# Squares, low parts and picks reordered between the last attention projection and the first expert

## The chip, the cores and the metric

The program runs on one core of one Trainium2 chip. The metric is the device time of one execution in microseconds (us), lower is better. A timed run starts the program once; the number quoted is the median of the runs.

## What is computed

A two-layer decoder over 512 tokens of width 1024. Layer 0 is a gated short convolution with a dense SwiGLU, layer 1 is latent attention with a mixture of eight experts, two for each token. The change stands where layer 1's attention ends and its experts begin; cut to that:

```python
x = x + mla_mixer(...)                      # ends with  o @ w_o
h = rmsnorm(x, norm_ffn[1])                 # x * rsqrt(mean(x*x) + eps) * g
probs = softmax(h @ router)                 # 8 logits per token
vals, idx = top_k(probs, 2)
gates = vals / sum(vals), scattered to (token, expert)
out = 0
for e in range(8):
    out = out + gates[:, e:e+1] * ((silu(h @ w_gate[e]) * (h @ w_up[e])) @ w_down[e])
x = x + out
```

## The kernel before, in words

Everything from line 404 on runs under a manual schedule: the order in which the code is written is the order in each engine's queue, and every engine works off its queue strictly in that order.

**Weights as chunks.** A class `Stream` brings the weights in as chunks of 128x2048 fp32 (1 MB each, `w_raw`, loaded by SP's queue into a ring of buffers). ScalarE (ACT) copies a chunk to a high part, `w_hi` (`split_hi`, L88), and VectorE (DVE) subtracts it from the raw chunk to get a bf16 low part, `w_lo` (`split_lo`, L97). A raw buffer is free for the next load once its low part is made. The first expert chunk alone, chunk 0, is split in eight pieces of 256 columns by the generator `pieces` (`split`, L117 on ACT and L120 on DVE), one piece for each pass of the loop below.

**The last output projection** (loop over `fo`, L877 to L895). `xT` holds x transposed, eight blocks of 128 features by 512 tokens. In each pass TensorE makes six products into a PSUM tile (`out_mm`, L688 to L690) and, two passes behind, the router's logits from the high and low parts `xhr` and `xlr` of that block (`logits`, L872 and L873). DVE adds the product to `xT` (L882), ACT copies it to `xhr` (L885), DVE makes the previous block's `xlr` (L888), ACT squares the block into `sq` (L891), GpSimd (POOL) adds the square to `acc` (L893), and one piece of chunk 0 is split. The last square is added by DVE behind the loop (L933).

**The router and the rows.** TensorE transposes `xT` back to rows of tokens, eight groups `rows_mm(0)` to `rows_mm(7)` (L909), the last ones placed between the router's steps. Each group is copied as it is to SBUF and stored to `out` (`base`, L921 and L922) and, scaled by the norm `r3`, split in a high part on ACT and a low part on DVE (`rows_ev`, L914 and L915; the tiles are called xh and xl in the profile). The norm comes from `acc`: TensorE sums over features (`pss`, L942), DVE makes `m4` (L1137), POOL raises it to the power -1/2 (L248). The logits are copied by ACT (`lgt`, L932), transposed on TensorE (L938) and ranked on DVE (L1139 to L1149) to the mask `sel`; products of `sel` with a triangular matrix (L1151, L1153) give each token's place in its expert (`pos`, L1159), and DVE turns expert 0's places into a one-hot matrix `oh1` (L1168). `keep_warm(n)` (L946) issues n products of ones that nobody reads.

**Picks.** For the first expert the tokens are picked by products: `pick(f, part)` (L1185 to L1190) multiplies the rows' high part (part 0) or low part (part 1) of feature block f with `oh1`, four products each, into one PSUM tile for each f. ACT and DVE evict it to `xe` (L1200, L1201). The PSUM pool `ops` has six buffers, shared by the loop's tiles, the rows and the picks, so a pick may have to wait until an older tile is read out. The later experts fetch their rows from memory (`hrow`), which POOL's queue writes (L1181).

**The experts** (L1319 on). Each chunk k gives 16 products with `w_hi` and 16 with `w_lo` (L1033). In the pass of chunk k, DVE first adds the two halves of the result (L1041) and then makes the low part of chunk k+2, besides the small work of ranking the experts and finding their rows.

## Time and profile before

| what | value |
|---|---|
| median of 3 runs | 1410.83 us (1410.05 to 1412.65) |
| the profiled execution | 1413.99 us |
| its span, first to last instruction | 1412.2 us |
| TensorE busy | 1378.1 us, 98% of the span |
| DVE busy | 991.5 us, 70% |
| ACT busy | 814.8 us, 58% |
| POOL busy | 281.2 us, 20% |
| mean granted TensorE clock | 0.993 of 2.4 GHz |

The span is the profiled execution from its first instruction to its last; the run's time has 1.8 us more around it. Busy shares are averages over all stages, and TensorE counts as busy while products follow each other, whatever its clock. The stage of the change is some 40 us of the 1412: the loop from 751 to 771 us, the router and the picks from 771 to 787, and the first chunks of the first expert behind it.

### The profile page before, as it was taken

Reading aid. Unit: us, or ns where it says so; the run is one execution under the profiler, and the core shown is the slowest. Engines: PE = TensorE matmul, PEld = TensorE weight load, DVE = VectorE, ACT = ScalarE, POOL = GpSimd, SP = SyncE. Lnnn points to the kernel's source line nnn. Section 1 sums busy time; section 2 is a strip of 40 time slices with the busy share of each in tenths; the row PEclk is TensorE's granted clock in tenths of the full one; section 3 lists DMA queues with packets and bytes.
Section 4 is the critical chain, followed back from the end, with each engine's and each line's share of the span. In section 5 each row is a group of like instructions: output and inputs, shape, how many; then the busy total and the mean of one; then the engine's idle time right before and its main releaser. Section 6 shows DMA issues by size and latency. Waiting matters only on the chain. (4 is left out here: it accounts for less than half of the span.)

```text
span 1412.2 us, 23783 instructions
## 1 busy us (share of the span) xinstructions
PE 1378.1 (98%) x9541; PEld 1198.7 (85%) x9544; DVE 991.5 (70%) x1263; ACT 814.8 (58%) x1210; POOL 281.2 (20%) x206
## 2 busy tenths in 40 slices
PE   9999999999999999999998999999999999999995
PEld 6888888888888887878876899999999999979893
DVE  7745564443344444586778897897979899999995
ACT  6323332221222233576645787877878788888892
POOL 0000000000000000143202432342523343443221
PEclk9999999999999999999999999999999999999998
DMA  6322223222232222111204999988999899999992
GB/s 222 135 92 90 90 90 119 90 90 90 95 114 90 90 90 92 64 35 58 91 0 162 309 366 370 311 324 289 357 321 343 340 348 368 318 399 359 402 375 70
DMA packets 49390, 284.40 MB, mean 201 GB/s; under 512 B 9320, under 2 KB 11112, under 8 KB 17272
## 3 DMA queue, kind: packets, MB, share of 16 engines
q1 hardware_dynamic: 41688, 269.82, 52.5%
q0 software_dynamic: 7584, 12.98, 3.9%
q8 instruction: 77, 1.26, 0.4%
q14 instruction: 41, 0.34, 0.1%
HBM read 271.39 MB, written 11.37 MB: 200 GB/s over the span
## 5 line engine op out<-in xcount | busy, mean ns | idle before, releaser
L97 DVE TENSOR_TENSOR w_lo<-w_raw,w_hi 128x2048 bf16<-128x2048 f32 (+1 forms) x239 | 555.7, 2326 | 54.2 <-ACT w_hi L88 54.2
L88 ACT CAST w_hi<-w_raw 128x2048 fp32r<-128x2048 f32 x239 | 456.4, 1910 | 216.3 <-PE ps L256 153.8
L1033 PE MATMUL gu<-xe,w_hi 128*128 128x304 f32 (+6 forms) x2048 | 288.8, 293 | 0.0
L1033 PEld LDWEIGHTS gu<-xe,w_hi 128*128 128x128 f32 x2048 | 264.0, 189 | 0.4
L255 PE MATMUL ps<-xh,w_hi 128*128 128x512 f32 x592 | 231.7, 391 | 1.6 <-DVE xT L399 0.9
L256 PE MATMUL ps<-xl,w_hi 128*128 128x512 f32 x592 | 230.5, 389 | 0.3 <-DVE xl L291 0.3
L257 PE MATMUL ps<-xh,w_lo 128*128 128x512 f32 x592 | 230.4, 389 | 0.0
L1047 POOL TENSOR_TENSOR sg<-sg,p 128x304 f32<-128x304 f32 (+6 forms) x64 | 93.8, 1465 | 310.8 <-ACT sg L1046 310.5
L1033 PE MATMUL gu<-xb,w_lo 128*128 128x152 bf16 (+6 forms) x2048 | 143.4, 223 | 3.8 <-DVE w_lo L97 3.7
L255 PEld LDWEIGHTS ps<-xh,w_hi 128*128 128x128 f32 x592 | 111.2, 188 | 26.0 <-ACT xh L290 1.4
L256 PEld LDWEIGHTS ps<-xl,w_hi 128*128 128x128 f32 x592 | 111.1, 188 | 24.3 <-DVE xl L291 0.8
L1033 PEld LDWEIGHTS <-w_lo 128*128 128x128 bf16 x2048 | 120.6, 98 | 12.8 <-DVE w_lo L97 5.6
L257 PEld LDWEIGHTS ps<-xh,w_lo 128*128 128x128 f32 x592 | 111.1, 188 | 23.1
L248 POOL TENSOR_TENSOR rs<-m,mhalf 128x4 f32<-128x4 f32 x3 | 3.1, 1019 | 589.2 <-DVE m L505 554.3
L1077 PE MATMUL gu<-ae,w_hi 128*128 128x304 f32 (+3 forms) x640 | 97.4, 302 | 0.0
L257 PE MATMUL ps<-ah,w_lo 128*128 128x512 f32 x240 | 94.7, 394 | 0.0
L256 PE MATMUL ps<-al,w_hi 128*128 128x512 f32 x240 | 94.6, 394 | 0.0
L255 PE MATMUL ps<-ah,w_hi 128*128 128x512 f32 x240 | 94.6, 394 | 0.0
L1077 PEld LDWEIGHTS gu<-ae,w_hi 128*128 128x128 f32 x640 | 87.1, 189 | 0.0
L1040 ACT COPY p<-gu 128x304 f32<-128x304 f32 (+6 forms) x128 | 49.1, 384 | 41.9 <-PE gu L1033 41.0
L1041 DVE TENSOR_TENSOR p<-gu,p 128x304 f32<-128x304 f32 (+6 forms) x128 | 55.5, 434 | 24.9 <-ACT p L1040 22.8
L968 POOL TENSOR_SCALAR oh<-rest,posn 128x152 bf16<-128x152 f32 (+6 forms) x28 | 58.0, 2084 | 1.3 <-DVE posn L1258 1.3
(334 smaller groups left out, 1875.9 us busy)
## 6 DMA issues: line engine op xcount, KB each, us to landing
w_raw<-w_moe SPq DMA_DIRECT2D x192, 1024.0 KB, 8.3
w_raw<-w_a SPq DMA_DIRECT2D x50, 1024.0 KB, 4.9
w_raw<-w_hp SPq DMA_DIRECT2D x4, 1088.0 KB, 5.9
w_raw<-w_o SPq DMA_DIRECT2D x4, 1024.0 KB, 4.7
xT<-xT_in SPq DMA_DIRECT2D x8, 256.0 KB, 4.8
out<-hs SPq DMA_DIRECT2D x8, 256.0 KB, 3.6
hrow<-xh POOLq DMA_DIRECT2D x2, 1024.0 KB, 5.9
hrow<-xl POOLq DMA_DIRECT2D x2, 1024.0 KB, 23.3
```

Source lines behind the costliest of these rows:

```text
L88: self.nc.scalar.copy(hi[:, :w], self.raw[k][:, :w])
L97: self.nc.vector.tensor_tensor(lo[:, :w], self.raw.pop(k)[:, :w], self.hi[k][:, :w].bitcast(F32), ALU.subtract)
L248: nc.gpsimd.tensor_tensor(out_t, m, h, ALU.pow)
L255: mm(ps, wh, xh[:, kc, :], start=kc == 0, stop=False)
L256: mm(ps, wh, xl[:, kc, :], start=False, stop=False)
L257: mm(ps, wl, xh[:, kc, :], start=False, stop=kc == n - 1)
L968: nc.gpsimd.tensor_scalar(s.oh[:, tb, 0:s.cap], iota[:, 0:s.cap], p[:, tb], None, op0=ALU.is_equal)
L1033: mm(s.ps[:, i, 0:n], w[:, b:b + P], x[:, kc], start=w is hi and kc == 0, stop=w is lo and kc == NB - 1)
L1040: nc.scalar.copy(p2, s.ps[:, :, s.cap:2 * s.cap])
L1041: tt(p2, s.ps[:, :, 0:s.cap], p2, ALU.add)
L1047: nc.gpsimd.tensor_tensor(s.sg, s.sg, s.p2[:, :, 1], ALU.mult)
L1077: mm(s.dp[q // 2][:, q % 2, 0:n], w[:, b:b + P], x[:, 4 * kq + j], start=w is hi and kq + j == 0, stop=w is lo and kq + j == 6)
```

## The change

It rewrites the order of this stage, in these edits:

1. In the loop the squares are added to `acc` by DVE and no longer by POOL. The eight pieces of chunk 0 are split to their high part alone (`split_hi_parts`); its low part is made in one operation behind the picks, ahead of chunk 1's.
2. The norm's sums stand ahead of the transposes of the logits. The copies `base(2)` and `base(3)` go from DVE to ACT; `rows_mm(4)` and `rows_mm(5)` move later.
3. Of twelve idle products three are left; those behind the products of `sel` are gone.
4. The picks run two feature blocks ahead and no longer one; `rows_ev(0)` goes ahead of `pos`, rows 7 and the rest of the rows behind the first two picks. ACT's high part of chunk 1 and the copies `base(4)` to `base(7)` stand together behind the last `rows_ev`. POOL's selection for expert 0 moves behind the first two stores to `hrow`, and `find(0)` one chunk later.

```diff
-    def split(self, parts=None, lag=False):
+    def split_hi_parts(self, parts):
...
+        for n in parts:
+            self.nc.scalar.copy(hi[:, a:a + n], self.raw[k][:, a:a + n])
+            a += n
+            yield
...
-    pieces = ws.split([256] * 8, True)
+    pieces = ws.split_hi_parts([256] * 8)
...
         if 0 < fo < NB - 1:
-            nc.gpsimd.tensor_tensor(acc, acc, sq, ALU.add)
-        if fo < NB - 1:
-            next(pieces)
+            tt(acc, acc, sq, ALU.add)
+        next(pieces)
...
-    rows_mm(4)
+    tt(acc, acc, sq, ALU.add)
+    for tb in range(TB):
+        t_s = slice(tb * P, (tb + 1) * P)
+        mm(pss[:, tb:tb + 1], acc[:, t_s], ones[:, 0:1], start=tb == 0, stop=tb == TB - 1)
     for i in range(2):
         base(i, nc.scalar.copy)
     lgt = ot.tile([2 * NE, T], F32, name="lgt", bufs=1)
     nc.scalar.copy(lgt, plt[0:2 * NE, :])
-    tt(acc, acc, sq, ALU.add)
-    for i in range(2, 4):
-        base(i, nc.vector.tensor_copy)
-    list(pieces)
     for tb in range(TB):
         nc.tensor.transpose(misc[:, tb * 2 * NE:(tb + 1) * 2 * NE], lgt[:, tb * P:(tb + 1) * P],
...
-    rows_mm(5)
+    for i in range(2, 4):
+        base(i, nc.scalar.copy)
+    rows_mm(4)
...
-    keep_warm(6)
-    ws.split_hi()
-    for i in range(4, 6):
-        base(i, nc.scalar.copy)
+    keep_warm(3)
...
     ts(sel_b, rank, 2.0, None, op0=ALU.is_lt)
+    rows_ev(0)
...
-    keep_warm(6)
+    rows_mm(5)
     rows_mm(6, idle)
...
-    ex[0].select(pos[:, :, 0:1])
...
-    for i in range(8):
+    for i in range(1, 4):
         rows_ev(i)
-        if i == 0:
-            rows_mm(7)
-    for i in (6, 7):
-        base(i, nc.scalar.copy)
...
     pick(0, 0)
+    pick(1, 0)
+    rows_mm(7)
+    for i in range(4, 8):
+        rows_ev(i)
+    ws.split_hi()
+    for i in range(4, 8):
+        base(i, nc.scalar.copy)
...
+        if part == 0:
+            ex[0].select(pos[:, :, 0:1])
     for f in range(NB):
-        if f < NB - 1:
-            pick(f + 1, 0)
+        if f < NB - 2:
+            pick(f + 2, 0)
         pick(f, 1)
...
+    ws.split_lo()
     ws.split_lo()
     ws.split_hi()
...
+                if c == 2:
+                    x.find(0)
                 if c == 1:
-                    x.find(0)
```

Three places of the engines' queues, before and then after. The first is DVE at the end of the loop over `fo`, from the sixth pass to the norm's `m`. Before:

```order
L120 TENSOR_TENSOR w_lo<-w_raw,w_hi 128x256 [waits Activation_49]
L882 TENSOR_TENSOR xT<-ps,xT 128x512 [waits PE_49]
L888 TENSOR_TENSOR xlr<-xT,xhr 128x512 [waits Activation_49]
L896 TENSOR_TENSOR xlr<-xT,xhr 128x512 [waits Activation_49]
L933 TENSOR_TENSOR acc<-acc,sq 128x512 [waits Activation_49,Pool_49]
L921 COPY hs<-ps 128x512 [waits PE_49] x2
L120 TENSOR_TENSOR w_lo<-w_raw,w_hi 128x256
L120 TENSOR_TENSOR w_lo<-w_raw,w_hi 128x256 [waits Activation_49]
L1137 TENSOR_SCALAR m_5915<-misc 128x4 [waits PE_49]
```

And now:

```order
L900 TENSOR_TENSOR acc<-acc,sq 128x512 [waits DVE_49,Activation_49]
L889 TENSOR_TENSOR xT<-ps,xT 128x512 [waits PE_49]
L895 TENSOR_TENSOR xlr<-xT,xhr 128x512 [waits DVE_49]
L902 TENSOR_TENSOR xlr<-xT,xhr 128x512 [waits Activation_49]
L934 TENSOR_TENSOR acc<-acc,sq 128x512 [waits Activation_49]
L1138 TENSOR_SCALAR m_5890<-misc 128x4 [waits PE_49]
```

The piece of `w_lo` between two additions to `xT` is gone, and in its place stands the addition to `acc`, which waits for ACT's square of the same pass; the two copies and the last two pieces behind the loop are gone as well.

The second place is ACT and TensorE from the rows to the picks. ACT before, from the high part of chunk 1 to the first eviction of a pick:

```order
L88 CAST w_hi<-w_raw 128x2048 [waits DMAHW4_49]
L921 COPY hs<-ps 128x512 [waits PE_49] x2
L914 ACTIVATE xh_5911<-ps,r_5916 128x512 [waits Pool_49]
L914 ACTIVATE xh_5911<-ps,r_5916 128x512
L914 ACTIVATE xh_5911<-ps,r_5916 128x512 [waits DVE_49] x2
L914 ACTIVATE xh_5821<-ps,r_5916 128x512 x2
L914 ACTIVATE xh_5821<-plt,r_5916 128x512 [waits PE_49]
L914 ACTIVATE xh_5821<-ps,r_5916 128x512 [waits PE_49]
L921 COPY hs<-plt 128x512 [waits DMAHW0_49,DVE_49]
L921 COPY hs<-ps 128x512 [waits DMAHW1_49,DVE_49]
L1200 ACTIVATE xe<-ps,vec 128x152 [waits PE_49,Activation_49]
```

And now, from the logits' copy on:

```order
L941 COPY lgt<-plt 16x512 [waits PE_49]
L927 COPY hs<-ps 128x512 x2
L920 ACTIVATE xh_5886<-ps,r_5891 128x512 [waits Pool_49]
L920 ACTIVATE xh_5886<-ps,r_5891 128x512 x3
L920 ACTIVATE xh_5815<-ps,r_5891 128x512 [waits PE_49] x2
L920 ACTIVATE xh_5815<-plt,r_5891 128x512 [waits PE_49]
L920 ACTIVATE xh_5815<-ps,r_5891 128x512 [waits PE_49]
L88 CAST w_hi<-w_raw 128x2048 [waits DMAHW4_49]
L927 COPY hs<-ps 128x512 [waits DVE_49] x2
L927 COPY hs<-plt 128x512 [waits DMAHW0_49,DVE_49]
L927 COPY hs<-ps 128x512 [waits DMAHW1_49,DVE_49]
L1206 ACTIVATE xe<-ps,vec 128x152 [waits PE_49,Activation_49]
```

The high part of chunk 1 (`w_hi`) has moved from ahead of the rows' high parts to behind them, and four copies `hs`, no longer two, stand between it and the first `xe`. TensorE before, from rows 6 to the fourth pick:

```order
L909 MATMUL plt<-ident,xT 128x128 x4
L909 MATMUL ps<-ident,xT 128x128 [waits DVE_49]
L909 MATMUL ps<-ident,xT 128x128 x3
L1189 MATMUL ps<-oh_5948,xh_5911 128x152 [waits DVE_49]
L1189 MATMUL ps<-oh_5948,xh_5911 128x152 [waits Activation_49] x3
L1189 MATMUL ps<-oh_5948,xh_5911 128x152 [waits DVE_49]
L1189 MATMUL ps<-oh_5948,xh_5911 128x152 x3
L1189 MATMUL ps<-oh_5948,xl_5912 128x152 x3
L1189 MATMUL ps<-oh_5948,xl_5912 128x152 [waits DVE_49]
L1189 MATMUL ps<-oh_5948,xh_5911 128x152 x4
L1189 MATMUL ps<-oh_5948,xl_5912 128x152 x4
L1189 MATMUL ps<-oh_5948,xh_5911 128x152 [waits DVE_49,PE_49]
```

And now, from the first pick on (xh_5886 and xl_5887 are the first half of the rows' high and low parts, xh_5815 the second half of the high parts):

```order
L1175 MATMUL ps<-oh_5920,xh_5886 128x152 [waits DVE_49,Activation_49] x4
L1175 MATMUL ps<-oh_5920,xh_5886 128x152 [waits DVE_49]
L1175 MATMUL ps<-oh_5920,xh_5886 128x152 x3
L915 MATMUL ps<-ident,xT 128x128 [waits DVE_49]
L915 MATMUL ps<-ident,xT 128x128 x3
L1175 MATMUL ps<-oh_5920,xh_5886 128x152 [waits DVE_49]
L1175 MATMUL ps<-oh_5920,xh_5886 128x152 x3
L1175 MATMUL ps<-oh_5920,xl_5887 128x152 x4
L1175 MATMUL ps<-oh_5920,xh_5886 128x152 [waits PE_49,Activation_49]
L1175 MATMUL ps<-oh_5920,xh_5886 128x152 x3
L1175 MATMUL ps<-oh_5920,xl_5887 128x152 x4
L1175 MATMUL ps<-oh_5920,xh_5815 128x152 [waits PE_49,Activation_49]
```

The first two picks stand ahead of rows 7 now. The wait of the pick behind the first `xl` products, the one of block 3, is on ACT: its PSUM buffer is that of rows 4, which `base(4)` is the last to read. The next one waits for `base(5)` in the same way.

The third place is DVE behind the last eviction of the picks. Before:

```order
L1201 SCALAR_TENSOR_TENSOR xe<-ps,vec,xe 128x152 [waits Activation_49] x8
L97 TENSOR_TENSOR w_lo<-w_raw,w_hi 128x2048 [waits DMAHW4_49]
L1208 TENSOR_TENSOR lg<-lg,mx_5942 128x32
L1209 TENSOR_TENSOR lg<-lg,r_5916 128x32 [waits DVE_49]
L1212 TENSOR_TENSOR gts<-lg,sel 128x32 [waits Activation_49]
```

And now:

```order
L1207 SCALAR_TENSOR_TENSOR xe<-ps,vec,xe 128x152 [waits Activation_49] x8
L108 TENSOR_TENSOR w_lo<-w_raw,w_hi 128x2048 [waits DMAHW3_49]
L108 TENSOR_TENSOR w_lo<-w_raw,w_hi 128x2048 [waits DMAHW4_49]
L1215 TENSOR_TENSOR lg<-lg,mx_5970 128x32 [waits DVE_49]
L1216 TENSOR_TENSOR lg<-lg,r_5891 128x32 [waits DVE_49]
```

Two whole low parts, of chunk 0 and of chunk 1, stand there in place of one.

## Rows read from the trace of the kernel before

**Rows 1.** The page's first part: busy us of each engine, its share of the span, and its instructions.

```profile
PE 1378.1 (98%) x9541; PEld 1198.7 (85%) x9544; DVE 991.5 (70%) x1263; ACT 814.8 (58%) x1210; POOL 281.2 (20%) x206
```

**Rows 2.** The timeline of DVE in the last output projection, 751 to 771 us. Columns: start in us, us busy, engine, line, operation, output and inputs, shapes, how many merged; in brackets the idle time ahead of it and what ended that.

```profile
753.17 0.69 DVE L882 TENSOR_TENSOR xT<-ps,xT 128x512 f32<-128x512 f32 x1 [0.68 <-PE ps L690]
...
763.52 0.68 DVE L882 TENSOR_TENSOR xT<-ps,xT 128x512 f32<-128x512 f32 x1
764.12 0.67 DVE L888 TENSOR_TENSOR xlr<-xT,xhr 128x512 fp32r<-128x512 f32 x1
...
765.65 1.72 DVE L888 TENSOR_TENSOR xlr<-xT,xhr 128x512 fp32r<-128x512 f32 x1
...
768.71 0.68 DVE L882 TENSOR_TENSOR xT<-ps,xT 128x512 f32<-128x512 f32 x1
```

**Rows 3.** The timeline of ACT from that loop to the router, same columns.

```profile
764.23 0.62 ACT L885 CAST xhr<-xT 128x512 fp32r<-128x512 f32 x1 [2.22 <-DVE xT L882]
764.75 0.63 ACT L891 ACTIVATE sq<-xT 128x512 f32<-128x512 f32 x1
...
769.95 0.63 ACT L891 ACTIVATE sq<-xT 128x512 f32<-128x512 f32 x1
770.48 1.05 ACT L921 COPY hs<-ps 128x512 f32<-128x512 f32 x2
771.42 0.57 ACT L932 COPY lgt<-plt 16x512 f32<-16x512 f32 x1
771.89 0.40 ACT L117 CAST w_hi<-w_raw 128x256 fp32r<-128x256 f32 x1
772.20 1.89 ACT L88 CAST w_hi<-w_raw 128x2048 fp32r<-128x2048 f32 x1
```

**Rows 4.** The timeline of POOL: one of its six adds of squares, same columns.

```profile
765.52 1.30 POOL L893 TENSOR_TENSOR acc<-acc,sq 128x512 f32<-128x512 f32 x1 [2.21 <-ACT sq L891]
```

**Rows 5.** The timeline of TensorE: two products of the loop, then from the router to the first expert's first product, same columns (the output's and the weights' partitions stand ahead of the shapes).

```profile
762.46 0.40 PE L688 MATMUL ps<-xh,w_hi 128*128 128x512 f32 x1
762.69 0.39 PE L689 MATMUL ps<-xl,w_hi 128*128 128x512 f32 x1
...
772.04 0.42 PE L938 MATMUL misc<-ident,lgt 16*128 16x16 f32 x4 [0.39 <-ACT lgt L932]
772.39 1.05 PE L942 MATMUL misc<-ones,acc 128*128 128x1 f32 x8
...
774.09 2.77 PE L949 MATMUL plt<-ones_b 128*128 128x512 bf16 x6
776.65 0.24 PE L1151 MATMUL misc<-sel,tri 128*128 128x40 bf16 x1
...
776.83 1.46 PE L949 MATMUL plt<-ones_b 128*128 128x512 bf16 x6
...
779.67 1.33 PE L1189 MATMUL ps<-oh,xh 128*128 128x152 f32 x8
...
781.29 0.61 PE L1189 MATMUL ps<-oh,xh 128*128 128x152 f32 x4
781.74 0.61 PE L1189 MATMUL ps<-oh,xl 128*128 128x152 f32 x4
...
787.43 2.58 PE L1033 MATMUL gu<-xe,w_hi 128*128 128x304 f32 x16
```

**Rows 6.** Busy time by stretches of half a microsecond: stretch, its length, busy us (and instructions) of PE, PEld, DVE, ACT, POOL; then the granted TensorE clock as a share of 2.4 GHz, the DMA share and GB/s.

```profile
773.00:773.50 0.50, 0.50 (x6) 0.50 (x7) 0.25 (x2) 0.50 (x1) 0.00 (x0) 0.94 1.05 373
...
774.00:774.50 0.50, 0.50 (x3) 0.18 (x2) 0.47 (x2) 0.50 (x3) 0.50 (x1) 0.50 0.98 369
776.50:777.00 0.50, 0.50 (x7) 0.28 (x6) 0.00 (x0) 0.50 (x2) 0.00 (x0) 0.65 1.83 397
```

**Rows 7.** The timeline of DVE from the router to the last rows, same columns as rows 2.

```profile
773.48 0.16 DVE L1137 TENSOR_SCALAR m<-misc 128x4 f32<-128x4 f32 x1 [0.25 <-PE misc L942]
...
775.18 0.18 DVE L1149 TENSOR_SCALAR sel<-rank 128x32 bf16<-128x32 f32 x1
...
777.24 1.06 DVE L1168 TENSOR_SCALAR oh<-rest,pos 128x152 fp32r<-128x152 f32 x4
778.22 4.03 DVE L915 SCALAR_TENSOR_TENSOR xl<-ps,r,xh 128x512 fp32r<-128x512 f32 x6
```

**Rows 8.** The timeline of ACT: the first six high parts of the rows, and a copy of rows to SBUF.

```profile
774.96 3.52 ACT L914 ACTIVATE xh<-ps,r 128x512 fp32r<-128x512 f32 x6
...
782.94 0.59 ACT L921 COPY hs<-plt 128x512 f32<-128x512 f32 x1 [2.55 <-DVE xl L915]
```

**Rows 9.** The timeline of DVE in the first expert: the low parts of chunk 1 and of chunk 6, and the first small operation behind the former.

```profile
788.35 2.28 DVE L97 TENSOR_TENSOR w_lo<-w_raw,w_hi 128x2048 bf16<-128x2048 f32 x1
790.54 0.18 DVE L1208 TENSOR_TENSOR lg<-lg,mx 128x32 f32<-128x32 f32 x1
...
809.68 2.27 DVE L97 TENSOR_TENSOR w_lo<-w_raw,w_hi 128x2048 bf16<-128x2048 f32 x1
```

**Rows 10.** Who waited for whom from 788.4 to 812 us, DVE alone: engine, output, line, what it waited for, then us in total, times, longest.

```profile
DVE gts L1212 <- ACT lg L1210: 0.3, 1, 0.3
```

**Rows 11.** The timeline of TensorE in the first expert: chunk 6, its high and its low products.

```profile
808.63 2.48 PE L1033 MATMUL gu<-xe,w_hi 128*128 128x304 f32 x16
812.01 1.23 PE L1033 MATMUL gu<-xb,w_lo 128*128 128x152 bf16 x16 [0.90 <-DVE w_lo L97]
```

More of the change, by code (lines that the diff above doesn't have):

```diff
@@ L99, in split_lo, with split @@
         self.n_lo += 1
-    def split(self, parts=None, lag=False):
+    def split(self, parts=None):
         if parts is None:
@@ L113, in split @@
         self.n_lo += 1
-        a, last = 0, None
-        for n in (*parts, 0) if lag else parts:
-            if n:
-                self.nc.scalar.copy(hi[:, a:a + n], raw[:, a:a + n])
-            if last or not lag:
-                s = last if lag else slice(a, a + n)
-                self.nc.vector.tensor_tensor(lo[:, s], raw[:, s], hi[:, s].bitcast(F32), ALU.subtract)
-            last = slice(a, a + n)
+        a = 0
+        for n in parts:
+            s = slice(a, a + n)
+            self.nc.scalar.copy(hi[:, s], raw[:, s])
+            self.nc.vector.tensor_tensor(lo[:, s], raw[:, s], hi[:, s].bitcast(F32), ALU.subtract)
             a += n
-            if n:
-                yield
+            yield
     def chunk(self):
@@ L939, in hybrid_trunk_kernel @@
                             ident[0:2 * NE, 0:2 * NE])
-    for tb in range(TB):
-        t_s = slice(tb * P, (tb + 1) * P)
-        mm(pss[:, tb:tb + 1], acc[:, t_s], ones[:, 0:1], start=tb == 0, stop=tb == TB - 1)
-    rows_mm(5)
+    for i in range(2, 4):
+        base(i, nc.scalar.copy)
+    rows_mm(4)
     idle = lps.tile([P, T], F32, name="plt")
@@ L1192, in hybrid_trunk_kernel @@
     pick(0, 0)
+    pick(1, 0)
[5 more added lines that the diff above has]
+        base(i, nc.scalar.copy)
+    cnt = cpool.tile([P, NE], F32, name="cnt")
+    nc.vector.tensor_copy(cnt, pc[:, TB, :])
+    mx = ot1([P, TB], "mx4")
+    nc.vector.tensor_reduce(mx, lg, axis=AX.X, op=ALU.max)
+    xe2 = ep.tile([P, NB, 2, 2, CAP], F32R, name="xe", bufs=1)
+    xb2 = ep.tile([P, NB, 2, CAP], BF16, name="xb", bufs=1)
+    ex[0].hold()
+    for part, op in enumerate((ALU.bypass, ALU.add)):
+        for hf in range(2):
+            nc.gpsimd.dma_start(hrow.rearrange("(t p) d -> p t d", p=P)[:, :, hf * T:(hf + 1) * T],
+                                tr[part][hf].bitcast(F32), accum_op=op)
+        if part == 0:
+            ex[0].select(pos[:, :, 0:1])
     for f in range(NB):
-        if f < NB - 1:
-            pick(f + 1, 0)
+        if f < NB - 2:
+            pick(f + 2, 0)
         pick(f, 1)
```

16 lines of the change are left out of this document (5 added, 11 removed).

## The prediction, made before the changed kernel was run

> **What bounds the kernel now.** I read the busy times first: TensorE is busy for 1378.1 us of the span [rows 1], so there are some 34 us to be won in all. Next I read the timelines of DVE, ACT and TensorE through the stage of the change, then the waits behind it. Three things in them matter.
>
> In the loop DVE never rests: additions to `xT` stand at 763.52 and 768.71, two passes apart, 2.60 us each [rows 2]. TensorE's eight products a pass, 0.23 us apart [rows 5], need 1.84. `xlr` takes 0.67 us alone and 1.72 us when POOL's add of squares (1.30 us) runs beside it [rows 2, 4].
>
> From the router on a chain sets the time: sums, `m` at 773.48, `sel` at 775.18, products of `sel` at 776.65, `oh1` from 777.24, rows, picks from 779.67, first expert product at 787.43 [rows 5, 7]. The products of `sel` could have begun at 775.4, but stood behind six idle products which took 2.77 us [rows 5].
>
> Behind the picks DVE is the bound. From 788.4 to 812 us it waits 0.3 us in all [rows 10], and in chunk 6 TensorE waits for DVE: high products from 808.63, low ones only at 812.01, 0.90 us idle ahead of them [rows 11].
>
> **The change, part by part.**
>
> *The loop.* A pass loses one piece of `w_lo` and POOL's adds; DVE gains the add. DVE's own work is then three operations issued 0.60 us apart (763.52 to 764.12 [rows 2]), 1.8 us. But the add waits for the square of its own pass, and the next `xT` stands behind the add. That makes a ring: `xT` to the copy `xhr` 0.71 us, to the square 0.52, the square itself 0.63 [rows 2, 3], the add's issue 0.60, and a few hundredths to wake DVE: 2.5 us a pass against 2.6. From `xT` of pass 1 at 753.17 [rows 2], the first whole ring ends at 755.7 and five more put the last `xT` at 768.2 where it was 768.71: **0.5 us won**. Had nothing but the lock between POOL and DVE been in the way, a pass would fall to TensorE's 1.84 us: that is a rival below.
>
> The Trainium skill's page SBUF — State Buffer, section "Who interferes with whom", states that a DVE operation with two SBUF inputs and a GpSimd operation that reads SBUF exclude each other for a whole instruction; the trace agrees, 0.67 against 1.72 us. By that rule alone one would credit the loop with 1.05 us for each clash that goes; by the ring of waits it gets 0.5 in all.
>
> *Norm and router.* The last square begins at 768.2 + 0.71 + 0.52 = 769.4, the last add ends about 770.8, and the sums (eight steps of 0.11, from 772.39 to the next work [rows 5, 7]) end at 771.8. They now run while ACT gets to the logits: from the square 0.53 to the next operation, a high piece at 0.31, two copies at 0.47 each, then `lgt` with 0.57 [rows 3]: 771.8. Transposes 0.35 [rows 5], so `m` stands at 772.3, not 773.48: **1.2 us earlier**. `sel` follows 1.70 us behind [rows 7], ready at 774.2, and nothing idle is in front of its products: 774.2 for 776.65. The two copies moved to ACT run from 771.7 to 772.8 and are hidden behind POOL's power of `m`, so they cost nothing; without that cover they would cost 1 us.
>
> *Rows and picks.* The rows' high parts started 1.48 us behind `m` [rows 7, 8], with ACT just done with other copies; now they start that much behind it or a little less, at 773.7. DVE makes the first `xl` ahead of `pos`, so `pos` comes at 775.1 and `oh1` is whole at 776.4 (1.06 us [rows 7]). The first pick can run then, 3.3 us earlier than at 779.67. What is late next is the PSUM buffers. The second pick, rows 7 and the third pick wait for `xl` 1, 2 and 3, 0.66 us apart (4.03 us for six [rows 7]): 777.1, 777.8, 778.4. With the first block's `xl` products TensorE is through at 779.3. The fourth pick then waits for `base(4)`, and ACT has rows 7's high part (0.57) and the whole high part of chunk 1 (1.80 [rows 3]) ahead of it: rows 7 are there at 778.2, the high part of chunk 1 goes from 779.0 to 780.8, `base(4)` takes 0.59 [rows 8], **781.4**. So 2 us of the gain end in a new wait. From there 12 half picks are left at 0.45 us (781.29 to 781.74 [rows 5]): 5.4 us, first expert product at **786.8**, 0.65 us earlier than 787.43.
>
> The clock is the second unknown. Before, it fell from 2.4 to 1.2 GHz in the stretch that begins at 773.0, was at half at 774.0, and rose again after 776.5, with the six idle products behind it [rows 6]; at half clock those took 2.77 us, at full clock the other six 1.46 [rows 5]. Now there are three and TensorE has little between 770.8 and 776.4, so I expect a fall, and it may still be low at the first picks. At double price the first two and a half blocks end at 780.7, still before `base(4)`; rows 7 and so `base(4)` come 0.8 us later, 782.2, and the first expert product at 787.55. Bounds for this part: -0.65 (clock high) and +0.1 us (low until 780.7); I take the middle, **-0.3**.
>
> *The low part of chunk 0.* In the loop its pieces cost nothing any more, but DVE now makes it whole behind the last `xe`, 2.19 us from issue to issue (788.35 to 790.54 [rows 9]), before everything that it did there until now. `find(0)` moves by one chunk, but stays ahead of chunk 6, and the rest is the same list. With 0.3 us of rest in 23.6 [rows 10] the list has no room: the low part of chunk 6 (809.68 [rows 9]) ends 2.2 us later as counted from the end of the picks, and since TensorE already waited for that one [rows 11], its low products come 2.2 us later. The stalls are spread, the first at chunk 0 itself: its low part ends some 3.2 us behind the first product, its sixteen high products take about 2.4 [rows 5, 9], so 0.8 us. From chunk 7 on DVE has room again, as before, but what TensorE lost stays lost. **+2.2**; bounds 0 (if DVE's list had slack that the waits do not show) and 2.7 (a clash with POOL's selections more). The load of chunk 6 waits for this low part now, until about 790; TensorE wanted that chunk at 808.6 [rows 11], so I cost it at nothing; past that cover it would add its lateness.
>
> **Sum.** -0.3 (loop, router and picks together, as one chain to the first expert product) + 2.2 = **+1.9 us**. The profiled execution of 1413.99 would become 1415.9. It is 3.2 us above the median of the runs, so I put the difference on the median: 1410.83 + 1.9 = **1412.7 us**, its own range 1411.9 to 1413.6.
>
> **The rivals.**
>
> *A, as above*: 55 in 100. 1412.7 us.
>
> *B, slower: the clock stays low through the picks.* In the low-clock case TensorE idles between 780.7 and 782.2, right behind the first picks, and if it has not got the full clock back by then, the twelve half picks cost 0.90 each until it does; at six of them 2.7 us, and DVE's list starts later by all of it: 1410.83 + 0.1 + 2.7 + 2.2 = 1415.8. For it: fewer idle products and a new idle stretch. Against it: once `oh1` is there TensorE has products without a gap until 780.7, and behind six idle products without a gap the clock rose before [rows 5, 6]. It decides from two half picks at the low clock behind 782 on. 20 in 100. The Trainium skill's page TensorE: Matmul & The Clock Gate, Part 1, states that the low clock is the default and that activity lifts it; the rows agree.
>
> *C, the low part costs nothing.* If DVE catches up before chunk 6, only the chain's -0.3 is left: 1410.5. Against it stand [rows 10, 11]. 12 in 100.
>
> *D, faster: the squares do not hold the loop.* If the loop falls to TensorE's 1.84 us a pass, the last `xT` comes at 764.2, 4 us earlier, and the router's chain with it: 1412.7 - 4.0 = 1408.7; with C 1406.5. For it: the lock cost DVE 1.05 us each time [rows 2]. Against it: the order of the three operations, of which the add must wait for ACT. 13 in 100.
>
> **How the numbers follow.** About 0.2%, 2.8 us, is what a measurement of this kernel can tell from no change. A, C and most of D lie within it: 68 in 100. Slower by more: B, with 1 in 10 of A's upper end, less what of B stays under: 23. Faster by more: a third of D and its case with C, and an error of mine in the chain: 9. The range goes from D's 1408.9 to B's 1415.6 and leaves out about 1 in 10 on either side.
>
> **What would show it.** In the changed profile: additions to `xT` 2.5 us apart, DVE's wait ahead of each add on ACT's square; `m` about 1.2 us earlier against the loop's end less 0.5; a wait of TensorE of some 2 us at the fourth pick, on ACT's copy of rows 4; the first expert product within 0.7 us of where it stood; a wait for `w_lo` at chunk 0 of 0.8 us; and the low products of chunk 6 more than 2 us later against the first expert product (24.58 us there before [rows 5, 11]). Wrong it would be if the loop's passes fell below 2.3 us, if the clock were low behind 782, or if chunk 7 began no later than before.

## The result, and the profile after

The changed kernel takes **1418.03 us** (median of 6 runs, 1415.31 to 1418.44) where the kernel before takes 1410.66 (6 runs of the same comparison): a ratio of 1.0052, 95% interval 1.0041 to 1.0063, **slower by 7.4 us**. The forecast was 1412.7, its range ended at 1415.6. The profiled execution takes 1418.44 us, its span is 1416.7. It reaches the loop 1.33 us earlier than the profile of before (addition to `xT` of pass 1 at 751.84, not 753.17), so places are compared by their distance from that addition or from the last one. A half pick, below, is the four products of one part of one feature block.

The loop and the router, DVE, answering to [rows 2, 7]; columns as there:

```profile
751.84 0.69 DVE L889 TENSOR_TENSOR xT<-ps,xT 128x512 f32<-128x512 f32 x1 [0.69 <-PE ps L697]
...
753.75 0.69 DVE L900 TENSOR_TENSOR acc<-acc,sq 128x512 f32<-128x512 f32 x1 [0.62 <-ACT sq L898]
754.36 0.69 DVE L889 TENSOR_TENSOR xT<-ps,xT 128x512 f32<-128x512 f32 x1
```

And from the norm on:

```profile
771.08 0.16 DVE L1138 TENSOR_SCALAR m<-misc 128x4 f32<-128x4 f32 x1 [1.49 <-PE misc L943]
...
772.78 0.18 DVE L1150 TENSOR_SCALAR sel<-rank 128x32 bf16<-128x32 f32 x1
```

A pass is 2.52 us, and ahead of each addition to `acc` DVE waits 0.62 us for ACT's square. Counted from pass 1, `m` and the products of `sel` come 0.1 to 0.15 us later than forecast, the first pick 0.65 us earlier. TensorE from there to chunk 7, answering to [rows 5, 11]:

```profile
773.02 0.19 PE L1153 MATMUL misc<-sel,tri 128*128 128x40 bf16 x1 [0.74 <-DVE sel L1150]
...
774.42 0.94 PE L1175 MATMUL ps<-oh,xh 128*128 128x152 f32 x4 [0.19 <-DVE oh L1166]
...
778.10 1.05 PE L1175 MATMUL ps<-oh,xl 128*128 128x152 f32 x4
780.59 1.13 PE L1175 MATMUL ps<-oh,xh 128*128 128x152 f32 x4 [1.43 <-ACT hs L927]
781.52 1.05 PE L1175 MATMUL ps<-oh,xl 128*128 128x152 f32 x4
...
788.35 2.76 PE L1175 MATMUL ps<-oh,xl 128*128 128x152 f32 x12
790.91 3.31 PE L1034 MATMUL gu<-xe,w_hi 128*128 128x304 f32 x16
794.20 1.23 PE L1034 MATMUL gu<-xb,w_lo 128*128 128x152 bf16 x16
```

```profile
814.20 2.49 PE L1034 MATMUL gu<-xe,w_hi 128*128 128x304 f32 x16
817.86 1.23 PE L1034 MATMUL gu<-xb,w_lo 128*128 128x152 bf16 x16 [1.16 <-DVE w_lo L108]
...
819.50 2.48 PE L1034 MATMUL gu<-xe,w_hi 128*128 128x304 f32 x16
```

The first pick runs at 774.42, 22.6 us behind pass 1 where it was 26.5. The fourth pick waits 1.43 us for ACT's copy. But then half picks follow each other in 0.86 us, not 0.45, until the first expert product at 790.91; and chunk 6 waits 1.16 us for its low part. The granted clock by stretches, answering to [rows 6] (PEclk is the third number from the right):

```profile
770.00:775.00 5.00, 4.07 (x34) 3.14 (x33) 3.62 (x13) 4.11 (x9) 1.01 (x1) 1.00 0.96 306
775.00:780.00 5.00, 3.90 (x18) 3.52 (x17) 4.68 (x9) 3.95 (x6) 2.41 (x3) 0.57 0.85 326
780.00:785.00 5.00, 4.41 (x21) 4.41 (x21) 1.01 (x3) 3.06 (x8) 3.35 (x5) 0.50 1.01 375
785.00:790.00 5.00, 5.00 (x25) 5.00 (x25) 1.01 (x4) 1.86 (x4) 1.29 (x1) 0.50 1.09 195
790.00:795.00 5.00, 5.00 (x34) 4.78 (x34) 4.04 (x5) 3.29 (x4) 0.00 (x0) 0.72 1.12 205
```

The clock fell between 775 and 780, stood at half, 1.2 GHz, through all twelve half picks, and rose about 792.8, under the first expert's products. Before, it had been back at 777 [rows 6].

So where the 7.4 us came from, by the two traces: the loop gives 0.46 us (15.08 for 15.54 from pass 1 to pass 7); from the last addition to `xT` to the first expert product it is 23.99 for 18.72 us, **5.27 lost**; from there to chunk 7's first product 28.59 for 26.23, **2.36 lost**. Together +7.17. The two profiled executions as wholes differ by less, 4.45 us, because that of before took 1.33 us more ahead of the loop and 1.3 us more behind chunk 7.

### The profile page after: what moved, and what is told of

It reads as the page before. It is cut to its first block, busy times and chain, and to the rows that moved or that the text cites. A ratio compares the mean times of both kernels' runs of the same rounds, so it can differ in the third digit from the quotient of the medians.

```text
span 1416.7 us, 23761 instructions
## 1 busy us (share of the span) xinstructions
PE 1380.6 (97%) x9534; PEld 1203.3 (85%) x9535; DVE 988.4 (70%) x1260; ACT 816.3 (58%) x1212; POOL 274.1 (19%) x200
## 3 DMA queue, kind: packets, MB, share of 16 engines
q8 instruction: 77, 1.26, 0.3%
```

## The experiments

F is the time from the last addition to `xT` to the first expert product, L from there to chunk 6's low products, both of the profiled execution; the clock is the mean granted one over the span, lowest and highest of the executions.

| run | median us (lowest to highest, executions) | kernel before, same comparison | F | L | clock |
|---|---|---|---|---|---|
| before | 1410.66 | | 18.72 | 24.58 | |
| changed | 1418.03 (1415.31 to 1418.44, 6) | 1410.66 | 23.99 | 26.95 | 0.989 to 0.991 |
| e1 idle back | 1415.88 (1413.78 to 1420.14, 9) | 1410.62 | 23.37 | 26.94 | 0.989 to 0.994 |
| e2 low early | 1414.81 (1413.57 to 1418.21, 12) | 1410.62 | 23.38 | 24.76 | 0.988 to 0.992 |
| e3 before, 3 idle | 1413.66 (1407.36 to 1416.37, 12) | 1410.62 | 17.46 | 24.58 | 0.988 to 0.995 |
| e4 e1 and e2 | 1413.91 (1410.70 to 1414.50, 12) | 1410.62 | 21.24 | 25.04 | 0.990 to 0.995 |
| e5 no stall | 1412.90 (1409.94 to 1416.47, 11) | 1410.64 | 22.34 | 26.96 | 0.988 to 0.997 |
| e6 e5 and idle | 1411.69 (1408.99 to 1414.50, 11) | 1410.64 | 16.90 | 27.91 | 0.994 to 0.997 |
| e7 e6, low in pieces | 1410.70 (1408.47 to 1414.92, 11) | 1410.64 | 16.89 | 27.06 | 0.992 to 0.997 |
| e8 idle in stall | 1411.83 (1410.71 to 1413.71, 11) | 1410.64 | 18.56 | 26.91 | 0.994 to 0.997 |
| e9 e7, high in pieces | 1408.69 (1407.25 to 1413.15, 12) | 1409.47 | 16.89 | 26.32 | 0.994 to 0.997 |
| e10 idle mid-picks | 1415.05 (1413.44 to 1416.69, 8) | 1409.47 | 22.40 | 26.92 | 0.990 to 0.996 |
| e11 before, low late | 1406.37 (1404.52 to 1408.33, 12) | 1409.47 | 18.22 | 26.77 | 0.995 to 0.997 |
| e12 squares on POOL | 1413.68 (1411.18 to 1416.88, 8) | 1409.41 | 24.99 | 26.99 | 0.986 to 0.992 |
| e13 all | 1407.06 (1404.32 to 1409.62, 11) | 1409.41 | 17.38 | 26.32 | 0.995 to 0.997 |
| e14 changed again | 1418.07 (1417.36 to 1419.21, 5) | 1409.41 | 23.39 | 26.95 | 0.988 to 0.992 |

The first four ask whether the clock and the late low part are separate losses, and what keeps the clock down.

**e1.** Twelve idle products again.

```diff
-    keep_warm(3)
+    keep_warm(6)
...
+    keep_warm(6)
     rows_mm(5)
     rows_mm(6, idle)
```

> The changed kernel with all twelve idle products back: six ahead of the router's ranking, six directly behind the products of sel. Theory 1 (the picks are slow because TensorE's clock stays at 1.2 GHz from 775.6 to 792 us of the changed profile, and what it lacks is activity around the router): the granted clock is near 1 through the half picks, these follow each other in 0.45 us and no longer 0.85; the idle products push rows 5 to 7 back by 1.5 to 2.8 us and with them the wait at the fourth pick by 0 to 2 us; the first expert product comes 3 to 4.5 us earlier than in the changed kernel and the time is 1413.5 to 1415 against 1418. Rival 1 (the half picks are held at 0.85 us by their evictions or PSUM buffers, not by the clock): half picks stay at 0.85 us, time 1418 to 1420. Rival 2 (the stall at the fourth pick alone brings the clock down): the clock falls again behind 779 and the time stays within 1 us of 1418.

2.1 us below the changed kernel. The clock held until 12.9 us behind the last addition to `xT`, the end of the wait at the fourth pick, then fell, and the half picks again took 0.85 us: rival 2 in this profile, though the time lies outside both forecasts. Whether the idle products moved the fall isn't shown: in the second profile of the changed kernel (e14) the clock held for 11.9 us and F is 23.39, as here.

**e2.** Chunk 0's low part ahead of the evictions.

```diff
+    ws.split_lo()
     for f in range(NB):
         if f < NB - 2:
...
-    ws.split_lo()
```

> The changed kernel with chunk 0's low part made ahead of the picks' evictions, in the 2.64 us in which DVE waited for the first xe; no other edit, clock as it is. Theory 2 (the low part behind the picks lengthens DVE's list by one operation of 2.2 us, and chunk 6 pays for it): first expert product within 0.3 us of the changed kernel's, low products of chunk 6 some 24.6 us behind it and no longer 26.95; time 2.0 to 2.4 us less than the changed kernel, about 1415.8. Rival (the 2.4 us at chunk 6 come from somewhere else, find(0) one chunk later or the slow clock): time within 0.5 us of 1418.

L falls from 26.95 to 24.76, **2.2 us**, as theory 2 has it; the time by 3.2. F is 0.6 lower too, but no lower than in e14's profile of the changed kernel: in both the clock fell 11.9 us behind the last addition, not 8.8. TensorE, the first expert product and chunk 6, whose wait is down from 1.16 to 0.59 us:

```profile
790.19 3.44 PE L1034 MATMUL gu<-xe,w_hi 128*128 128x304 f32 x16
...
814.95 1.23 PE L1034 MATMUL gu<-xb,w_lo 128*128 128x152 bf16 x16 [0.59 <-DVE w_lo L108]
```

**e3.** The kernel before with three idle products.

```diff
-    keep_warm(6)
+    keep_warm(3)
...
-    keep_warm(6)
     rows_mm(6, idle)
```

> The kernel before with three idle products of twelve, as in the changed kernel, and nothing else changed: no wait at the fourth pick, picks one ahead. If the missing idle products alone keep the clock low: half picks at 0.85 to 0.90 us from 779 on, first expert product 4 to 7 us later than before, time 1415 to 1418 against 1410.7. If it is the stall at the fourth pick that keeps the clock low: the clock is back within the first picks, first expert product between 1 us earlier and 1.5 us later, time 1409.7 to 1412.

Neither alone, but both in turn: five executions took 1407.36 to 1407.98 us at a mean clock of 0.995, seven 1413.43 to 1416.37 at 0.988 to 0.991, none between. The profile is one of the first five; its clock fell ahead of the picks and was back in time, and F is 1.26 us below before. Nearly all of that is what three more idle products cost at half clock: the products of `sel` come 6.70 us behind the last addition (772.37 to 765.67), before 7.94 [rows 2, 5]. The six behind `sel` cost nothing, since from its products to the first expert product it is 10.76 us here and 10.78 before. TensorE's timeline:

```profile
770.92 1.49 PE L949 MATMUL plt<-ones_b 128*128 128x512 bf16 x3
772.37 0.21 PE L1151 MATMUL misc<-sel,tri 128*128 128x40 bf16 x1
```

Its stretches:

```profile
770.00:772.00 2.00, 2.00 (x11) 1.17 (x10) 1.65 (x6) 2.00 (x4) 1.02 (x1) 0.63 0.84 303
772.00:774.00 2.00, 1.63 (x10) 0.86 (x9) 1.66 (x10) 2.00 (x5) 1.00 (x2) 0.52 0.93 302
774.00:776.00 2.00, 1.29 (x8) 0.94 (x8) 2.00 (x4) 2.00 (x5) 2.00 (x4) 1.00 0.92 272
```

So where the clock falls and returns differs from one execution of a kernel to the next, and the idle products buy fewer bad ones: with all twelve, one of 32 executions of the kernel before in the same comparison took over 1413.4 us, with three it is seven of 12.

**e4.** e1 and e2 together.

```diff
-    keep_warm(3)
+    keep_warm(6)
...
+    keep_warm(6)
     rows_mm(5)
...
+    ws.split_lo()
     for f in range(NB):
...
-    ws.split_lo()
```

> The changed kernel with both edits, twelve idle products and chunk 0's low part ahead of the evictions. If the two losses are separate they add: e1's gain of 3 to 4.5 plus e2's gain of 2.0 to 2.4 us, time 1411 to 1413. If the slow clock only covered for the late low part (chunk 0's products slower, so that the low part was waited for less), the sum is larger by up to 0.9 us: 1410.5.

2.0 us below e1 and 0.9 below e2, less than expected: the clock still fell in the picks, 15.4 us behind the last addition in this profile, so that only the last six half picks and part of one more were slow.

The next four take the pause away, fill it, or both.

**e5.** ACT's high part of chunk 1 moves from ahead of `base(4)` to the middle of the evictions.

```diff
-    ws.split_hi()
     for i in range(4, 8):
         base(i, nc.scalar.copy)
...
+        if f == 3:
+            ws.split_hi()
     ws.split_lo()
```

> The changed kernel with ACT's high part of chunk 1 moved from ahead of base(4) to the middle of the picks' evictions, so that the fourth pick need not wait; three idle products as in the changed kernel. Theory 1 as it stands after the first four runs (what brings the clock down for the rest of the picks is a pause of TensorE between the router and the picks, whichever it is): the wait of 1.4 to 1.9 us at the fourth pick is gone. If the small waits around the first picks (0.74, 0.19, 0.26 us) already bring the clock down, as in the changed kernel's profile, where it fell ahead of the long wait: half picks still at 0.85 us, first expert product some 21.5 us behind the last addition to xT and no longer 24.0, time about 1415.5. If only the long wait does it: half picks at 0.45 us, first expert product at 16.5 to 17 us, time 1410 to 1412, and a wait of about 0.8 us for chunk 0's low part comes out.

The wait is gone, but in the profile the clock fell as in the changed kernel, 8.6 us behind the last addition, with no idle time of TensorE over 0.74 us in these 8.6, and gapless picks from 774.1 to 787.7 ran at half clock. TensorE's timeline:

```profile
785.17 2.76 PE L1175 MATMUL ps<-oh,xl 128*128 128x152 f32 x12
787.73 3.92 PE L1034 MATMUL gu<-xe,w_hi 128*128 128x304 f32 x16
```

The granted clock in it (PEclk, third from the right):

```profile
778.00:783.00 5.00, 5.00 (x25) 5.00 (x25) 1.27 (x5) 1.95 (x6) 3.90 (x5) 0.50 1.00 372
783.00:788.00 5.00, 5.00 (x25) 5.00 (x25) 1.50 (x4) 3.83 (x7) 1.29 (x1) 0.50 1.07 190
```

Again both cases: six executions at 1409.94 to 1412.90 (clock 0.994 to 0.997), five at 1414.31 to 1416.47 (0.988 to 0.990).

**e6.** e5 and e1 together.

```diff
-    keep_warm(3)
+    keep_warm(6)
...
+    keep_warm(6)
     rows_mm(5)
...
-    ws.split_hi()
     for i in range(4, 8):
...
+        if f == 3:
+            ws.split_hi()
```

> The same, with twelve idle products. Theory 1: no pause of over 0.3 us is left from the loop to the first expert product, the clock stays at 1.0 in all of the stage, half picks 0.45 us, first expert product 16.5 to 17.5 us behind the last addition to xT; the late low part of chunk 0 still costs 2.2 to 3 us; time 1410 to 1411.5, with a smaller spread than the run before it. Rival (the slow clock is a matter of chance and of neither): the same spread as with three idle products, median above 1413.

All eleven executions are at 0.994 or more; F is 16.90, as forecast. 6.3 us below the changed kernel. L rose to 27.91, 3.3 above before where 2.2 to 3 were expected: with fast picks the late work shows, first the fifth eviction, behind ACT's 1.9 us high part, then chunk 0's low part. TensorE's timeline:

```profile
782.21 0.76 PE L1034 MATMUL gu<-xe,w_hi 128*128 128x304 f32 x4
783.40 2.38 PE L1034 MATMUL gu<-xe,w_hi 128*128 128x304 f32 x12 [0.43 <-DVE xe L1207]
786.46 1.23 PE L1034 MATMUL gu<-xb,w_lo 128*128 128x152 bf16 x16 [0.68 <-DVE w_lo L108]
```

**e7.** e6 with chunk 0's low part in eight pieces, one behind each eviction on DVE (`split_lo_parts` is `split_lo` by columns).

```diff
...
+    low0 = ws.split_lo_parts([256] * 8)
     for f in range(NB):
...
+        next(low0)
         if f == 3:
             ws.split_hi()
-    ws.split_lo()
     ws.split_lo()
```

> The same, and chunk 0's low part made in eight pieces, one behind each eviction of a pick on DVE (0.4 us of work in the 0.45 us in which DVE waits there). Theories 1 and 2: first expert product as in the run before, low products of chunk 6 some 24.6 us behind it, time 2.2 to 3 us below the run before: 1407.5 to 1409 against 1410.6, faster than both kernels. Rival (DVE's pieces push the evictions back and so the picks): first expert product 1 to 2 us later, time 1409 to 1411.

1.0 us instead of 2.2 to 3, and no faster than before. ACT's high part of chunk 1, 1.9 us, still stood among the evictions, DVE waited 1.54 us for the fifth, and the last began at 786.09, 2.6 us behind the picks' end. DVE's timeline:

```profile
784.23 0.38 DVE L1221 SCALAR_TENSOR_TENSOR xe<-ps,vec,xe 128x152 fp32r<-128x152 f32 x1 [1.54 <-ACT xe L1220]
...
786.09 0.37 DVE L1221 SCALAR_TENSOR_TENSOR xe<-ps,vec,xe 128x152 fp32r<-128x152 f32 x1
```

**e8.** The changed kernel with its wait, twelve idle products and eight more inside the wait (`cnt` is copied earlier, so that they may write the free columns of `misc`).

```diff
-    keep_warm(3)
+    keep_warm(6)
...
+    keep_warm(6)
     rows_mm(5)
...
     for f in range(NB):
+        if f == 1:
+            for _ in range(8):
+                mm(misc[:, 128:512], ones_b, ones_b[:, None, :].to_broadcast([P, 3, P]), start=True, stop=True)
```

> The changed kernel with its wait at the fourth pick, twelve idle products as before and eight more (384 columns, about 0.17 us each) inside that wait. Nothing is gained from the wait itself, so only the clock can change the time. Theory 1: half picks at 0.45 us and no longer 0.85, first expert product 18.5 to 19 us behind the last addition to xT against 23.4 with the twelve alone, time 1411 to 1413 against 1415.9 with the twelve alone. Rival (idle products do nothing for the picks' clock): time 1415 to 1417.

As theory 1 has it, and the cleanest price of the clock: the fourth pick still comes at 13.1 us behind the last addition, the same evictions and buffers follow, the half picks take 0.45 us, and the time is 4.1 us under e1, 6.2 under the changed kernel. So it was not evictions or buffers that held the half picks at 0.85 (e1's rival 1). TensorE's timeline, from the eight idle products to the first expert product:

```profile
776.44 1.48 PE L1203 MATMUL misc<-ones_b 128*128 128x384 bf16 x8
778.54 0.67 PE L1178 MATMUL ps<-oh,xh 128*128 128x152 f32 x4 [0.62 <-ACT hs L927]
779.04 0.61 PE L1178 MATMUL ps<-oh,xl 128*128 128x152 f32 x4
...
783.96 2.58 PE L1034 MATMUL gu<-xe,w_hi 128*128 128x304 f32 x16
```

The last six ask for the price of the rest.

**e9.** e7 with ACT's high part of chunk 1 in eight pieces as well.

```diff
+    hi1 = ws.split_hi_parts([256] * 8)
...
         next(low0)
-        if f == 3:
-            ws.split_hi()
+        next(hi1)
```

> The kernel of the run e7 with ACT's high part of chunk 1 in eight pieces too, one behind each eviction of a pick, in place of one operation of 1.9 us behind the fourth eviction. In e7 that operation held the fifth eviction from 780.8 to 783.8 us, so that the first expert product came with the picks' end at 16.9 us but its sixteen high products waited 1.1 us for evictions, and DVE's list began 2.6 us later than the picks allowed. Theory 2 (DVE's list from the last eviction to chunk 6 sets the time there): waits in chunk 0 gone, low products of chunk 6 some 41.5 to 42 us behind the last addition to xT (e7 43.95, before 43.3), time 1408 to 1409 against 1410.6 for the kernel before. Rival (pieces of ACT and DVE, 0.6 to 0.8 us a block with the evictions, are too much for picks of 0.9 us): first expert product later than 17.5 us, time 1410 or more.

The ratio to before is 0.9992 (0.9981 to 1.0002): no difference that shows. L is 26.32 still: DVE's low part of chunk 1 begins 2.5 us behind the first expert product (784.65 to 782.14), where it was 0.9 before [rows 5, 9]. Chunk 6's low products come 43.2 us behind the last addition, not 41.5 to 42 as expected, though the time lies where it was forecast. So the low part of chunk 0 can be hidden by the picks, but not for nothing at their full speed.

**e10.** The changed kernel with eight idle products in the middle of the picks (`cnt` is copied earlier, as in e8).

```diff
...
     for f in range(NB):
+        if f == 2:
+            for _ in range(8):
+                mm(misc[:, 128:512], ones_b, ones_b[:, None, :].to_broadcast([P, 3, P]), start=True, stop=True)
```

> The changed kernel (three idle products, the wait at the fourth pick in place) with eight idle products of 384 columns in the middle of the picks, behind the first four of twelve half picks. If dense products bring the clock back where the picks alone do not: the granted clock rises within the picks, the rest of the half picks go at 0.45 us, first expert product 1 to 3 us earlier than the 24.0 behind the last addition to xT of the changed kernel although the idle products take 1.3 to 2.6 us themselves; time 1415 to 1417. If it is only a matter of time until the clock returns: it returns where it did, some 25.5 us behind the last addition to xT, first expert product at 25.5 to 26.5, time 1419 to 1420.

The idle products ran at half clock for 2.3 us, the clock rose about 1 us behind them, 18.5 us behind the last addition and not 25.9, and from there the half picks are at full speed. The time, 1415.05, is as expected. That it is only a matter of time until the clock returns is unlikely by this profile: it was low for 6.8 us here, for 10.2 to 20.5 in the seven others that lost it there. TensorE's timeline:

```profile
780.13 2.78 PE L1202 MATMUL misc<-ones_b 128*128 128x384 bf16 x8
782.45 1.22 PE L1177 MATMUL ps<-oh,xh 128*128 128x152 f32 x4
783.48 0.71 PE L1177 MATMUL ps<-oh,xl 128*128 128x152 f32 x4
```

The granted clock in it:

```profile
780.00:782.00 2.00, 2.00 (x8) 1.05 (x8) 0.75 (x2) 0.42 (x2) 1.36 (x1) 0.50 1.01 381
782.00:784.00 2.00, 2.00 (x11) 1.77 (x10) 0.00 (x0) 0.00 (x0) 0.88 (x1) 0.58 1.23 286
784.00:786.00 2.00, 2.00 (x20) 2.00 (x20) 0.75 (x2) 1.24 (x3) 0.40 (x1) 1.00 0.87 154
```

**e11.** The kernel before with the late low part alone.

```diff
-    pieces = ws.split([256] * 8, True)
+    pieces = ws.split_hi_parts([256] * 8)
...
+    ws.split_lo()
     ws.split_lo()
```

> The kernel before with one part of the change alone: in the loop chunk 0 is split to its high part only, its low part is made whole behind the picks. Twelve idle products, squares on GpSimd, picks as before. Theory 2 at the full clock: loop and router within 0.5 us (a pass loses the low piece of 0.4 us but keeps the clash of xlr with the add of squares), a wait of 0.7 to 0.8 us for the low part at chunk 0, low products of chunk 6 26.8 to 27.9 us behind the first expert product against 24.58; time 2 to 3.3 us above the kernel before, 1412.6 to 1414. Rival (the loss at chunk 6 in the changed kernel comes from find(0) one chunk later): no change, 1410.6.

L rose by 2.19 us, the low end of what was expected, 0.66 of it at chunk 0. But the loop fell to TensorE's own time, 1.85 us a pass, 10.63 us for six passes and not 15.54, and the kernel is **faster than before: 0.9977 (0.9967 to 0.9987)**. I had expected 0.5 us from the loop at most, and 2 to 3.3 us more in all. By the profiles 4.91 us from the loop and 0.50 in F less the 2.19 are 3.2 us; the medians differ by 3.1. DVE waits for products now, and it is GpSimd's add, 1.30 us where `xlr` was the one to wait [rows 2, 4], that is stretched to 1.76 to 1.85 beside DVE, while `xlr` keeps its 0.68. DVE's timeline, and POOL's with the six adds in one row:

```profile
753.44 0.69 DVE L893 TENSOR_TENSOR xT<-ps,xT 128x512 f32<-128x512 f32 x1 [0.57 <-PE ps L701]
754.05 0.68 DVE L899 TENSOR_TENSOR xlr<-xT,xhr 128x512 fp32r<-128x512 f32 x1
755.29 0.69 DVE L893 TENSOR_TENSOR xT<-ps,xT 128x512 f32<-128x512 f32 x1 [0.56 <-PE ps L701]
```

The timeline of POOL:

```profile
752.18 11.11 POOL L904 TENSOR_TENSOR acc<-acc,sq 128x512 f32<-128x512 f32 x6 [42.45 <-ACT sq L902]
```

**e12.** The changed kernel with the squares on GpSimd again.

```diff
-            tt(acc, acc, sq, ALU.add)
+            nc.gpsimd.tensor_tensor(acc, acc, sq, ALU.add)
         next(pieces)
```

> The changed kernel with one edit undone: the squares are added by GpSimd again; chunk 0 still gives only its high part in the loop. Theory 3 (what held the loop at 2.5 us a pass is that DVE's add stands behind ACT's square of its own pass and ahead of the next addition to xT; without the low pieces of chunk 0 DVE has room, and GpSimd's add of 1.3 us need not meet xlr): passes of 1.85 us, TensorE's own time, as in the run e11; last addition to xT 10.6 to 11 us behind that of pass 1 and no longer 15.08; the norm 0.3 to 1.4 us later against it; the picks' slow clock as it was; time 3 to 4.5 us under the changed kernel of the same chip, about 1414. Rival (the lock between GpSimd and DVE comes back with GpSimd's adds and costs about 1 us at each xlr): passes of 2.5 to 2.6 us, no change.

**4.4 us** below the changed kernel on the same chip, with the clock still low in the picks. Passes of 1.85 us, 10.63 for six: DVE's add behind ACT's square is what held the changed kernel's loop. The norm comes 0.9 us later against the loop's end, as expected (0.3 to 1.4). DVE's timeline:

```profile
755.96 0.69 DVE L889 TENSOR_TENSOR xT<-ps,xT 128x512 f32<-128x512 f32 x1 [0.57 <-PE ps L697]
...
757.81 0.69 DVE L889 TENSOR_TENSOR xT<-ps,xT 128x512 f32<-128x512 f32 x1 [0.56 <-PE ps L697]
```

**e13.** e9 with the squares on GpSimd.

```diff
-            tt(acc, acc, sq, ALU.add)
+            nc.gpsimd.tensor_tensor(acc, acc, sq, ALU.add)
         next(pieces)
```

> The kernel of e9 (no wait at the fourth pick, twelve idle products, chunk 0's low part and chunk 1's high part in pieces between the evictions) with the squares on GpSimd. By theories 1 to 3 together: passes of 1.85 us, so 4.4 us from the loop less up to 1.4 us that the norm is later against its end; clock at 1.0 from the loop to the first expert product; chunk 6 as in e9. Time 1404 to 1405.7 where the kernel before has 1409.5 to 1410.6 and e11 had 1406.4. Rival (the loop's gain is lost at the sums, where GpSimd's last adds meet DVE): 1406.5 to 1408.

Faster than before, 0.9979 (0.9970 to 0.9988), but 1.4 us above what I expected, where the rival had it, and no better than the one part in e11. In its profile GpSimd and DVE fell into the other order from the third pass on, DVE waited, and six passes took 11.40 us, 0.77 more than in e12; F is 0.49 above e9's. So the larger part of the miss lies in the loop and not, as the rival had it, at the sums. The same two timelines:

```profile
753.54 0.68 DVE L908 TENSOR_TENSOR xlr<-xT,xhr 128x512 fp32r<-128x512 f32 x1
...
754.92 1.82 DVE L908 TENSOR_TENSOR xlr<-xT,xhr 128x512 fp32r<-128x512 f32 x1
...
757.26 1.17 DVE L908 TENSOR_TENSOR xlr<-xT,xhr 128x512 fp32r<-128x512 f32 x1
```

The timeline of POOL:

```profile
758.67 1.29 POOL L913 TENSOR_TENSOR acc<-acc,sq 128x512 f32<-128x512 f32 x1 [0.79 <-ACT sq L911]
```

**e14.** The changed kernel again.

> The changed kernel once more, as the other end of the comparison on the same chip: 1417 to 1418.5 in most executions, and in a few, where the clock comes back sooner or falls later, 1411 to 1415.

1418.07, 11.0 us above e13 and 4.4 above e12; the few faster executions that I expected did not come.

## Why the prediction was wrong

**Right by its steps.** The ring in the loop: passes of 2.52 us, 0.46 won for 0.5, the wait on ACT's square as described. The norm: `m` 19.24 us behind pass 1 for 20.31, 1.1 won for 1.2. `sel`'s products, 2.3 won for 2.45; the first pick, 3.9 for 3.3. The new wait of the fourth pick on `base(4)`: its place and cause, and 0.5 us later than the 781.4 worked out (28.75 us behind pass 1, not 28.23), the transposes `rows_mm(7)` having gone at half clock; where they went at full clock it came 13.1 us behind the last addition (e1, e8, e10, e14), and 13.2 had been worked out. At full clock the rest holds too: F is 18.56 in e8, and the forecast's chain has 18.6 (786.8 less 768.2). The late low part: +2.2 forecast, 2.36 in the changed trace, 2.2 by e2, 2.19 by e11. The 0.8 us forecast for chunk 0 did not show in the changed kernel, since its high products took 3.29 us at the low clock and covered it; in e6, e8 and e11, at full clock, it is 0.66 to 0.68.

**The step that failed** is "12 half picks are left at 0.45 us: 5.4 us", with its bound for a low clock "until 780.7". They took 10.32 us, 4.9 more, and that is nearly all of the 5.27 lost there. In the sum it is the term of -0.3 for loop, router and picks: it measured +4.8 (5.27 less 0.46). The mechanism stood there as rival B, with half the size (six of twelve, 2.7 us) and 20 in 100. What weighed against it was an inference from one execution: behind six idle products without a gap the clock rose, so picks without a gap should hold or lift it. They don't lift it. In the changed kernel and in e5 TensorE ran 10 to 14 us of picks without a pause at 0.50. In the eight profiles that lost the clock there, it came back 1 us behind idle products (e10) or 2 to 5 us into the first expert's products (the other seven). Nor do they always hold it: in e4 it fell among them, 2.4 us into picks without a pause. So twelve half picks were slow in six of these profiles (changed, e1, e2, e5, e12, e14), six and a part in e4, three in e10: rival B's six is one outcome of several, and the changed kernel took all twelve.

The page TensorE: Matmul & The Clock Gate of the Trainium skill, Part 1, calls the low clock the default that activity lifts; the rows agree with the default, and with the second half only in part: here the measurement decides, by which a TensorE shown busy all through, 5.00 us of 5.00 from 785 to 790, stayed at the low level. The same part says that the low clock at a kernel's start lasts through a different number of products from run to run; nothing here looks at the start, but e3 and e5 show the like in mid-kernel, two groups of executions whose medians lie 6.7 and 3.8 us apart.

**What brought the clock down.** Either of two things is enough in part of the executions: the missing idle products with no wait at the fourth pick (five of 11 in e5, seven of 12 in e3), and the wait with all idle products back (most of e1, by the mean clock). With both mended, or with the wait filled, the profiles show no fall there (e6 to e9 and e13), and of the 56 executions only one has a mean clock as low as 0.992 (e7). The mean clock can't rule out a short fall, since falls elsewhere lower it as well. Which moment it falls at in a given execution, 8.6 to 15.4 us behind the loop in these profiles, the runs don't settle; only one execution of each has rows.

**What the prediction had not seen.** It credited the removal of the low pieces and the move of the squares together with 0.5 us. The parts are far apart: the first alone is worth 4.9 us in the loop (e11), and the second gives 4.4 of them back (e12). It also counted the clash with GpSimd at half its size: not only `xlr` is stretched by it, at 1.05 us each time, but the piece of `w_lo` behind it too, 1.50 us for 0.41. DVE before:

```profile
764.72 0.41 DVE L120 TENSOR_TENSOR w_lo<-w_raw,w_hi 128x256 bf16<-128x256 f32 x1
...
767.29 1.50 DVE L120 TENSOR_TENSOR w_lo<-w_raw,w_hi 128x256 bf16<-128x256 f32 x1
```

Rival D named TensorE's pace as a possible end and rightly held against it the order of DVE's three operations, but not that this order was the doing of the change. The Trainium skill's page SBUF — State Buffer, section "Who interferes with whom", says that the order of issue decides which of GpSimd and DVE is blocked; e11 and e13 agree, with the add at 1.76 to 1.85 us and `xlr` at 0.68 in the one, the add at 1.29 and `xlr` at 1.17 to 1.82 in the other, where the add starts first (758.67 against 759.22).

**Its base.** The profile of before stood 3.2 us above the median. Its clock also fell at 599 to 603 and 633 to 637 us; profiles without these two falls reach pass 1 between 749.83 (e1) and 752.00 (e14), not at 753.17, so the falls are part of it at least. The difference was put on the median, so no step hung on it. The range's ends, 1408.9 and 1415.6, each lie 0.2 us inside the sums of D and B, 1408.7 and 1415.8.

## What to carry to other kernels

Before taking idle products away, or letting a new wait into a stretch of small products, price that whole stretch at the low clock: here it was 4.9 us against some 1.2 that three of the idle products cost at the low clock (e3). When an operation moves to a less loaded engine, ask what it waits for there and who stands behind it: the add of squares made a ring of 2.5 us out of a loop that TensorE could run in 1.85. Undo each part alone on the chip, since a change that is slower as a whole held one part that is worth 3 us (e11), and all the mended parts together were worth no more (e13).
